# A two-layer hybrid network on one core: the norm's rows on VectorE, the last block of W in halves, another end of the last pair, updates between the projection's products

## Chip, cores and metric

The kernel runs on one core of one Trainium2 chip. The metric is the device time of one execution in microseconds (us), the median of three runs for the kernel before.

## What is computed

The input is 512 tokens of width 2048 and float32 weights. There are two layers. The first (attention and a recurrent time mix) is not touched. The second is a gated MLP with a mix along the tokens in chunks of 128, and both layers end in a post-norm and a gated projection of a side input `p`:

```python
        else:
            proj = xn @ c_w_in[j]
            u, v, g = _split(proj, (GMLP_W, GMLP_W, GMLP_W))
            oc = chunked_spatial_gating(u, v, c_ln_g[j], c_ln_b[j], c_w_s[j], c_b_s[j])
            y = (oc * jax.nn.silu(g)) @ c_w_out[j]
        h = h + rms_norm(y, norm_post[i])
        h = h + (p[i] @ ple_w_proj[i]) * jax.nn.sigmoid(h @ ple_w_gate[i])
```

In `chunked_spatial_gating`, `v` goes through a gelu and a layer norm (mean and variance, then times `c_ln_g`, plus `c_ln_b`), and each of 16 groups of 128 channels is multiplied from the left by its own lower triangle `w_s`.

## The kernel before

**Numbers.** Each float32 operand is split into a rounded part and its rest (`hi`, `lo`, typed fp32r), and a product is three matmuls: hi·hi, hi·lo, lo·hi. For a piece of W this split is one ScalarE cast (`whi`, L1384) and one VectorE subtraction (`wlo`, L1385) of 128x512; four of each can be in flight (`wsp`, four buffers). TensorE takes them in order: L1412 and L1414 need `whi`, L1413 needs `wlo`.

**Seven products.** `c_w_in` (the parts V, U, G) and the last `ple_w_gate` are multiplied by a scheme of seven products of half size in place of eight. `Pair` is two neighbouring column blocks of 512; `seven` (L1393) runs a list of (pair, product). One product is 8 k-tiles x 2 row blocks x 3 = 48 matmuls of 128x128x512. `pieces` (L1324) makes the combination of W's four quarter blocks that each product needs, in four pieces j of 128x1024 (512 KB): products 1 and 2 load; 5 adds a block onto the pieces of product 1 (called E) by an accumulating DMA from GpSimd's queue (`grow`, L1341); 6 loads four new pieces (H) and VectorE adds them to E (`add`, L1345); 3 uses H; 4 loads the last block, W's lower left one, piece by piece (L1337) and adds it to E (L1345); 7 grows H. Pieces come from a queue of nine homes, `raws`: two of the pool `wraw`, seven tiles `rq0` to `rq6`. In product 4 the loaded piece goes back to the front of that queue (`gone(g, True)`).

The order is 1, 2, 5, 6, 3, 4, 7 for a pair. The two pairs of V and the two pairs of `ple_w_gate` (called a and b here) are interleaved by `FIRST`: b1, a1, b2, a2, a5, a6, a3, a4, a7, b5, b6, and then an end that is handed in: 3, 4, 7 for V and 7, 4, 3 for the last layer. Product 1 of b isn't kept there, so b5 loads and grows.

**Side work by ticks.** `tick` counts k-tiles; `later(n, step)` puts a step n ticks ahead. `mix(g, at)` (L1490) is the mix along the tokens of group g in the U and G stages: at -11 its loads by ScalarE's queue, at -5 `norm` (four ScalarE activations L1508, one GpSimd select L1511 on `w_s`, two GpSimd tensor_tensor L1512 and L1513 for the gain and shift rows, which are broadcast), at 0 `split` (cast L1523, subtraction L1524), at +4 `mul` (three matmuls L1529 to L1531 and the gating L1533).

**Last layer.** `post_norm` (L978) runs the products with `c_w_out`, calls `next(filler)`, takes the norm's factor (`rstdB`), and runs the rest of `filler`: four groups of `ple_w_proj`, 24 matmuls each, whose results go through one of four tiles (`sg`, `sq`, two buffers each) to DRAM (`pd`, L1140 and L1141). After it come `update(q, 0)` (L1149, L1150) for eight blocks of `h`, and the operand of product 1 (`part`, L959 and L960). `flip` transposes the new `h` back to rows, 16 times, through a `sg` tile to DRAM (`rd`, L1165 and L1166). `fetch` (L1207, L1208) loads `pd` and `rd` for `emit`, on SyncE's queue (SP), on which the loads of W stand too; its slots are reused after the output has been written (L1216).

A scheduler sets the order on each engine at build time from the program's order and priorities; the `wlo`, `whi` and `add` instructions have a high one. Each engine then executes its queue in order.

```python
            else:
                tl = done = pr.E.pop(j)
                g = load(1, 0, j)
                add(tl, g)
                self.gone(g, True)
```

## Time and profile before

| | |
|---|---|
| median of 3 runs | 2293.2 us (2292.34 to 2300.28) |
| profiled execution | 2295.81 us, its span 2294.0 us |
| TensorE busy | 2230.5 us (97%) |
| VectorE busy | 1485.0 us (65%) |
| ScalarE busy | 1226.0 us (53%) |
| GpSimd busy | 289.8 us (13%) |
| mean granted TensorE clock | 0.992 |
| stages from 1376 to 1895 us | V, U and G of `c_w_in` |
| 1895 to 2074 us | products with `c_w_out` |
| 2074 to 2101 us | `ple_w_proj`, updates of h |
| 2101 to 2285 us | the fourteen products with `ple_w_gate` |

How to read it: PE is TensorE, DVE VectorE, ACT ScalarE, POOL GpSimd, SP SyncE; a suffix q is the engine's instruction queue. The view by stages gives busy time of each engine in a stretch, then the granted TensorE clock, the busy share of the DMA engines and GB/s. The view of waits gives who waited for whom, in total, how often, and the longest. In the timeline stand start, duration, engine, line, operation, and in brackets the idle time before it with what ended it. In the view of groups stand busy time in total, mean ns of one, and the idle time before.

### The profile page before, as it was taken

The numbers are of one execution on the slowest core, as the hardware profiler recorded it, in microseconds if no ns is written. First come the engines' busy times: TensorE is split into PE (matmuls) and PEld (weight loads), VectorE is DVE, ScalarE is ACT, GpSimd is POOL, SyncE is SP. The second block draws the span as 40 slices with busy tenths as digits, with TensorE's granted clock in tenths as the row PEclk, the third lists the DMA queues.
The fourth block names the chain that finished last, engine by engine and source line by source line (L and its number), as shares of the span: only waits on it lengthen the run. The fifth ranks groups of instructions, "written<-read, shape, count | busy, mean of one in ns | idle before, by whom it ended". The sixth has DMA issues, their size and how long they took to land.

```text
span 2294.0 us, 38975 instructions
## 1 busy us (share of the span) xinstructions
PE 2230.5 (97%) x14787; PEld 1823.1 (79%) x14787; DVE 1485.0 (65%) x2821; ACT 1226.0 (53%) x2510; POOL 289.8 (13%) x334
## 2 busy tenths in 40 slices
PE   8999999999999999999999999999999999998988
PEld 7878888888887888878888888877877878887767
DVE  8666667766634878862246449777787784226878
ACT  5455555555444777753344447556655654335644
POOL 2000011010100000000110112112241220010020
PEclk9999999999999999999999999999999999999999
DMA  6322232223235533343335446876676774336696
GB/s 231 90 77 78 64 86 79 73 66 84 75 97 153 154 101 98 97 149 99 97 102 172 129 120 173 209 191 150 181 207 154 215 207 134 97 104 207 173 265 196
DMA packets 298969, 311.58 MB, mean 136 GB/s; under 512 B 14701, under 2 KB 198158, under 8 KB 297758
## 3 DMA queue, kind: packets, MB, share of 16 engines
q1 hardware_dynamic: 254878, 253.52, 36.2%
q0 software_dynamic: 17408, 33.56, 8.6%
q10 hardware_dynamic: 26496, 22.03, 3.2%
q8 instruction: 116, 1.90, 0.3%
q14 instruction: 71, 0.58, 0.1%
HBM read 274.15 MB, written 34.90 MB: 135 GB/s over the span
## 4 chain that ended last, share of the span: by engine, by line
PE 78%; DVE 9%; DMA 7%; ACT 3%; issue 3%; SPq 0%; POOL 0%; ACTq 0%; DVEq 0%; POOLq 0%
PE mm L195 11%; PE mm L197 11%; PE mm L196 11%; PE mm L981 6%; PE mm L983 6%; PE mm L982 6%; PE mm L1413 5%; PE mm L1414 5%; PE mm L1412 5%; DVE wlo L1385 3%; DMA rq<-in_ple_w_gate_dram 2%; PE tm L533 1%; DMA rd<-sg 1%; DVE rq L1345 1%; PE tm L554 1%
## 5 line engine op out<-in xcount | busy, mean ns | idle before, releaser
L181 DVE TENSOR_TENSOR wlo<-raw,whi 128x512 fp32r<-128x512 f32 x464 | 331.7, 722 | 423.5 <-ACT whi L179 384.7
L179 ACT CAST whi<-raw 128x512 fp32r<-128x512 f32 x464 | 287.2, 620 | 459.1 <-PE mm L982 227.8
L196 PE MATMUL mm<-xl,whi 128*128 128x512 f32 x1088 | 427.3, 393 | 0.0
L195 PE MATMUL mm<-xh,whi 128*128 128x512 f32 x1008 | 418.4, 415 | 0.0
L197 PE MATMUL mm<-xh,wlo 128*128 128x512 f32 x1008 | 398.1, 395 | 0.0
L1384 ACT CAST whi<-rq 128x512 fp32r<-128x512 f32 x336 | 206.7, 621 | 167.9 <-PE mm L1414 91.4
L1385 DVE TENSOR_TENSOR wlo<-rq,whi 128x512 fp32r<-128x512 f32 x336 | 241.6, 730 | 77.7 <-ACT whi L1384 77.2
L196 PEld LDWEIGHTS mm<-xl,whi 128*128 128x128 f32 x1088 | 205.4, 189 | 33.5
L197 PEld LDWEIGHTS mm<-xh,wlo 128*128 128x128 f32 x1008 | 189.4, 188 | 41.7
L195 PEld LDWEIGHTS mm<-xh,whi 128*128 128x128 f32 x1008 | 190.1, 189 | 33.9
L981 PE MATMUL mm<-yl,whi 128*128 128x512 f32 x336 | 130.9, 390 | 0.0
L983 PE MATMUL mm<-yl,wlo 128*128 128x512 f32 x336 | 130.7, 389 | 0.0
L1456 POOL TENSOR_TENSOR accq<-accq,sq 128x512 f32<-128x512 f32 x42 | 56.8, 1351 | 473.1 <-ACT sq L1454 472.0
L1413 PE MATMUL mm<-wlo,xl 128*128 128x512 f32 x256 | 103.0, 402 | 11.7 <-DVE wlo L1385 11.6
L982 PE MATMUL mm<-xl,whi 128*128 128x512 f32 x288 | 112.0, 389 | 0.0
L1413 PE MATMUL mm<-wlo,yl 128*128 128x512 f32 x256 | 101.4, 396 | 10.1 <-DVE wlo L1385 10.0
L1412 PE MATMUL mm<-whi,yl 128*128 128x512 f32 x256 | 102.1, 399 | 1.1 <-ACT comb L1423 0.9
L1412 PE MATMUL mm<-whi,xl 128*128 128x512 f32 x256 | 102.7, 401 | 0.0
L1413 PE MATMUL mm<-wlo,yh 128*128 128x512 f32 x256 | 100.0, 391 | 2.2 <-DVE wlo L1385 2.2
L1414 PE MATMUL mm<-whi,xl 128*128 128x512 f32 x256 | 102.1, 399 | 0.0
L1414 PE MATMUL mm<-whi,yh 128*128 128x512 f32 x256 | 99.9, 390 | 1.1 <-DVE yh L960 1.1
L1414 PE MATMUL mm<-whi,yl 128*128 128x512 f32 x256 | 101.0, 394 | 0.0
(489 smaller groups left out, 4707.9 us busy)
## 6 DMA issues: line engine op xcount, KB each, us to landing
raw<-in_ab_w_in_dram SPq DMA_DIRECT2D x128, 512.0 KB, 3.9
rq<-in_c_w_in_dram SPq DMA_DIRECT2D x75, 512.0 KB, 6.9
rq<-in_c_w_in_dram POOLq DMA_DIRECT2D x38, 512.0 KB, 7.9
raw<-in_ple_w_gate_dram SPq DMA_DIRECT2D x36, 512.0 KB, 3.9
rq<-in_ple_w_gate_dram SPq DMA_DIRECT2D x36, 512.0 KB, 5.3
raw<-in_ab_w_out_dram SPq DMA_DIRECT2D x32, 512.0 KB, 3.7
raw<-in_c_w_out_dram SPq DMA_DIRECT2D x32, 512.0 KB, 3.8
raw<-in_c_w_in_dram SPq DMA_DIRECT2D x25, 512.0 KB, 5.8
```

Source lines behind the costliest of these rows:

```text
L179: nc.scalar.copy(hi[:, : m * n], src)
L181: self.weng.tensor_tensor(lo[:, : m * n], src, f(hi[:, : m * n]), ALU.subtract)
L195: nc.tensor.matmul(acc, hi, xhi[k], start=(k == 0), stop=False)
L196: nc.tensor.matmul(acc, hi, xlo[k], start=False, stop=False)
L197: nc.tensor.matmul(acc, lo, xhi[k], start=False, stop=(k == nk - 1))
L981: nc.tensor.matmul(accs[j], hi[:, js], xhi[k], start=(k == 0), stop=False)
L982: nc.tensor.matmul(accs[j], hi[:, js], xlo[k], start=False, stop=False)
L983: nc.tensor.matmul(accs[j], lo[:, js], xhi[k], start=False, stop=(k == nk - 1))
L1385: nc.vector.tensor_tensor(lo, src, f(hi), ALU.subtract)
L1412: nc.tensor.matmul(acc[m], xh, hi, start=(first and r == 0), stop=False, **more)
L1413: nc.tensor.matmul(acc[m], xh, lo, start=False, stop=False, **more)
L1414: nc.tensor.matmul(acc[m], xl, hi, start=False, stop=(r == 7), **more)
```

## The change

1. `norm` in `mix`: the two tensor_tensor of the gain and shift rows go from GpSimd to VectorE; `norm` is put at -4 instead of -5, `mul` at +5 instead of +4.
2. Product 4 of every pair loads the last block of W as eight 128x512 halves (256 KB) into two tiles of their own, `half0` and `half1`, and adds each to its half of E. To make room, `raws` loses `rq6`: eight homes instead of nine.
3. The end of b is 4, 7, 3 instead of 7, 4, 3, and the `fetch` ahead of product 3 is put off by three ticks.
4. In `filler` the eight `update(q, 0)` and the four `part` calls come between the groups of `ple_w_proj`, the results of which go through eight tiles `xl0` to `xl7` instead of four. The flips of the first two row blocks go through `xl` tiles, the others through `sg` and `sq`; these others come at ticks 30 to 37 instead of 20 to 34, and three later steps move by one tick.

```diff
-            self.raws = deque([(self.wraw, "raw", 2)] * 2 + [(wq, f"rq{j}", 1) for j in range(7)])
+            self.raws = deque([(self.wraw, "raw", 2)] * 2 + [(wq, f"rq{j}", 1) for j in range(6)])
...
             for g in range(4):
+                if g == 1:
+                    self.A11 = self.whole_set()
+                for q in (2 * g - 2, 2 * g - 1) if g else ():
+                    update(q, 0)
+                    if q < 4:
+                        self.part(self.A11, q, H[q, 0])
                 accs = self.dense_tm(i["ple_w_proj"][1], g * T, T, phi, plo, ps)
                 for m in range(4):
-                    pj = self.t(wp, [P, T], ("sg", "sq")[m % 2])
+                    pj = self.slot("xl", 4 * (g % 2) + m, F32)
                     nc.scalar.copy(pj, accs[m])
                     nc.scalar.dma_start(self.pd[:, m, g * T : (g + 1) * T], pj)
                 if g == 0:
                     yield
+            for q in (6, 7):
+                update(q, 0)
...
-            o = self.t(wp, [P, T], "sg")
+            o = self.slot("xl", g + 4 * m, F32) if m < 2 else self.t(wp, [P, T], ("sg", "sq")[m % 2])
...
-        order = FIRST(*pairs, (7, 4, 3))
+        order = FIRST(*pairs, (4, 7, 3))
...
                 elif prod == 3:
-                    fetch(pr.n + 1, (0, 1))
+                    self.later(3, lambda: fetch(pr.n + 1, (0, 1)))
...
                 tl = done = pr.E.pop(j)
-                g = load(1, 0, j)
-                add(tl, g)
-                self.gone(g, True)
+                for a in range(2):
+                    g = self.t(self.wq, [P, T], f"half{a}")
+                    k = 8 + 2 * j + a
+                    nc.sync.dma_start(g, pr.W[k * P : (k + 1) * P, pr.c0 : pr.c0 + T])
+                    add(tl[:, a * T : (a + 1) * T], g)
...
-                nc.gpsimd.tensor_tensor(vn, vn, row(0), ALU.mult)
-                nc.gpsimd.tensor_tensor(vn, vn, row(1), ALU.add)
+                nc.vector.tensor_tensor(vn, vn, row(0), ALU.mult)
+                nc.vector.tensor_tensor(vn, vn, row(1), ALU.add)
...
-            for n, step in ((-11, load), (-5, norm), (0, split), (4, mul)):
+            for n, step in ((-11, load), (-4, norm), (0, split), (5, mul)):
```

From the changed lines on, line numbers move by up to three: `add` is L1346 after, `wlo` L1388, the norm's rows L1515 and L1516, `fetch` L1208 and L1209, the loads of W L1338 and, for the halves, L1380.

**VectorE in the first pair of U, products 6 and 3.** Before, product 6's last add (L1345, the first row) is followed by `wlo` of the pieces, and an add of 128x1024 for product 4 comes after every two to four of them:

```order
L1345 TENSOR_TENSOR rq_3514_17144<-rq_3514_17144,rq_3577_17420 128x1024
L1385 TENSOR_TENSOR wlo_17355<-raw_17078,whi_17354 128x512
L1385 TENSOR_TENSOR wlo_17365<-raw_17078,whi_17364 128x512
L1345 TENSOR_TENSOR raw_17078<-raw_17078,rq_3601_17532 128x1024
L1385 TENSOR_TENSOR wlo_17378<-raw_17100,whi_17377 128x512
L1385 TENSOR_TENSOR wlo_17388<-raw_17100,whi_17387 128x512
L1385 TENSOR_TENSOR wlo_17401<-rq_3509_17122,whi_17400 128x512
L1385 TENSOR_TENSOR wlo_17411<-rq_3509_17122,whi_17410 128x512
L1345 TENSOR_TENSOR raw_17100<-raw_17100,rq_3606_17555 128x1024
```

After, at the same place, adds of halves stand between, and the norm's rows (`sq`, L1515 and L1516):

```order
L1346 TENSOR_TENSOR rq_3507_17102<-rq_3507_17102,half_3609_17556 128x512
L1346 TENSOR_TENSOR rq_3507_17102<-rq_3507_17102,half_3610_17559 128x512
L1515 TENSOR_TENSOR sq_17731<-sq_17731,accq_17730 128x512
L1388 TENSOR_TENSOR wlo_17412<-rq_3512_17124,whi_17411 128x512
L1388 TENSOR_TENSOR wlo_17425<-rq_3517_17146,whi_17424 128x512
L1516 TENSOR_TENSOR sq_17731<-sq_17731,accq_17730 128x512
L1388 TENSOR_TENSOR wlo_17435<-rq_3517_17146,whi_17434 128x512
L1346 TENSOR_TENSOR rq_3512_17124<-rq_3512_17124,half_3615_17582 128x512
L1388 TENSOR_TENSOR wlo_17448<-rq_3522_17168,whi_17447 128x512
L1346 TENSOR_TENSOR rq_3512_17124<-rq_3512_17124,half_3616_17585 128x512
```

The rows L1515 and L1516 are new on this engine; between two uses of the same half tile stand three `wlo`, where between two uses of the piece for product 4 stood four.

**ScalarE at the end of the projection.** Before, the casts of product 1's operand (`xh`, L959) stand behind all sixteen copies (L1140) of the projection's results:

```order
L1140 COPY sq_21689<-mm_21649 128x512
L1140 COPY sg_21692<-mm_21650 128x512
L1141 DMA pd_101<-sq_21689 128x512
L1141 DMA pd_101<-sg_21692 128x512
L1140 COPY sq_21695<-mm_21651 128x512
L959 CAST xh_4491_21698<-yh_4263_20537 128x512
L1141 DMA pd_101<-sq_21695 128x512
L959 CAST xh_4491_21698<-yh_4269_20553 128x512
```

After, the first two stand behind four copies:

```order
L1151 COPY xl_4473_21609<-mm_21567 128x512
L1151 COPY xl_4474_21612<-mm_21568 128x512
L1152 DMA pd_101<-xl_4473_21609 128x512
L179 CAST whi_21748<-raw_21746 128x512
L1152 DMA pd_101<-xl_4474_21612 128x512
L959 CAST xh_4476_21620<-yh_4287_20609 128x512
L959 CAST xh_4476_21620<-yh_4293_20625 128x512
L179 CAST whi_21764<-raw_21746 128x512
```

The other two casts follow behind eight copies.

**SP in the last pair, around a7 and b5.** Before, the loads of W (`rq`) stand between single fetches of `rd`:

```order
L1216 DMA out_dram<-xh_4724_22559 128x512
L1208 DMA xh_4724_22559<-rd_102 128x512
L1337 DMA rq_4811_22988<-in_ple_w_gate_dram 128x2x512
L1208 DMA xh_4724_22559<-rd_102 128x512
L1337 DMA rq_4816_23011<-in_ple_w_gate_dram 128x2x512
L1337 DMA rq_4821_23034<-in_ple_w_gate_dram 128x2x512
```

After, both fetches stand ahead of the last load for b5 and the four for b6:

```order
L1217 DMA out_dram<-xh_4751_22644 128x512
L1338 DMA rq_4826_23021<-in_ple_w_gate_dram 128x2x512
L1209 DMA xh_4751_22644<-rd_102 128x512 x2
L1338 DMA rq_4831_23044<-in_ple_w_gate_dram 128x2x512
L1338 DMA rq_4839_23072<-in_ple_w_gate_dram 128x2x512
```

So the two fetches have changed their places with one load.

More of the change, by code (lines that the diff above doesn't have):

```diff
@@ L1093, in rest @@
                         self.part(A11, q, xs[q, 0])
-            wq = pool("wq", 1)
-            self.raws = deque([(self.wraw, "raw", 2)] * 2 + [(wq, f"rq{j}", 1) for j in range(7)])
+            wq = self.wq = pool("wq", 1)
+            self.raws = deque([(self.wraw, "raw", 2)] * 2 + [(wq, f"rq{j}", 1) for j in range(6)])
             self.rp = pool("rp", 3)
@@ L1132, in keep, with update @@
             return last
+        def update(q, e):
+            r = self.rstdB[:, e * 256 : e * 256 + 256].unsqueeze(1).broadcast_to([P, 2, 256])
+            nc.vector.tensor_tensor(Y[q, e], Y[q, e], r, ALU.mult)
+            nc.vector.tensor_tensor(H[q, e], H[q, e], Y[q, e], ALU.add)
         def filler():
@@ L1143, in filler @@
                     yield
+            for q in (6, 7):
+                update(q, 0)
         self.post_norm(i["c_w_out"][0], npost[:, 16:32], yops, keep, ps, wp, early, filler(), None, pre)
-        def update(q, e):
-            r = self.rstdB[:, e * 256 : e * 256 + 256].unsqueeze(1).broadcast_to([P, 2, 256])
-            nc.vector.tensor_tensor(Y[q, e], Y[q, e], r, ALU.mult)
-            nc.vector.tensor_tensor(H[q, e], H[q, e], Y[q, e], ALU.add)
-        A11 = self.whole_set()
-        for q in range(4):
-            update(q, 0)
-            self.part(A11, q, H[q, 0])
-        for q in range(4, 8):
-            update(q, 0)
         def flip(g, m):
@@ L1168, in last_layer @@
         sets, x2, less, s1, s24, s3 = self.sums(H, wp)
-        sets[1] = A11
+        sets[1] = self.A11
         for q in range(4):
@@ L1194, in last_layer @@
         steps += [(19 + 3 * q, lambda q=q: s24(q, less(q))) for q in range(4)]
-        steps += [(20 + 2 * k, lambda g=g, m=m: flip(g, m)) for k, (g, m) in enumerate((g, m) for g in (2, 0, 3, 1) for m in (2, 3))]
-        steps += [(37 + q, lambda q=q: s3(q)) for q in range(4)]
-        steps += [(42, x22), (46, late_spare)]
+        steps += [(30 + k, lambda g=g, m=m: flip(g, m)) for k, (g, m) in enumerate((g, m) for g in (2, 0, 3, 1) for m in (2, 3))]
+        steps += [(38 + q, lambda q=q: s3(q)) for q in range(4)]
+        steps += [(43, x22), (47, late_spare)]
         for n, step in steps:
```

## The prediction

> **What bounds the kernel now.** I read the page first (TensorE, PE, is busy 97% of the span), then the view by stages, to see where the other 3% lie.
>
> ```profile
> 1490.00:1895.00 405.00, 384.54 (x1669) 310.44 (x1668) 315.68 (x434) 236.51 (x429) 99.24 (x82) 0.98 0.72 186
> ...
> 2074.00:2101.30 27.30, 21.15 (x92) 16.84 (x90) 24.49 (x41) 16.43 (x30) 0.00 (x0) 0.98 0.76 246
> 2101.30:2180.00 78.70, 74.51 (x333) 59.48 (x334) 58.74 (x92) 50.28 (x90) 4.80 (x4) 0.94 0.63 184
> 2180.00:2285.40 105.40, 93.75 (x397) 75.48 (x396) 83.71 (x128) 48.97 (x84) 14.44 (x12) 0.97 0.88 243
> 2285.40:2294.00 8.60, 2.07 (x10) 1.37 (x8) 4.06 (x6) 1.16 (x2) 0.00 (x0) 0.85 0.16 61
> sum 2294.00, PE 2230.49 PEld 1823.05 DVE 1485.02 ACT 1226.05 POOL 289.82; mean PE 278.81 PEld 227.88 DVE 185.63 ACT 153.26 POOL 36.23
> ```
>
> The columns are width, busy time of PE, weight load, VectorE (DVE), ScalarE (ACT) and GpSimd (POOL), then the granted TensorE clock, the DMA engines' busy share, GB/s. A stage loses its width less PE's busy time, and with it (1 - clock) x width, matmuls that ran slow. So the 405 us of V's end, U and G (call it **a**) lose 20.5 + 8.1 = 28.6; the projection (**b**) 6.15 + 0.5 = 6.7; the first part of the gate's products (**c**) 4.2 + 4.7 = 8.9; the rest of them (**d**) 11.65 + 3.2 = 14.8; the tail (**e**) is 8.6 long and holds little matmul. The clock has two digits, which in a means 2 us either way. PE's work itself stays, so a gain can only come out of these 67.6 us (28.6 + 6.7 + 8.9 + 14.8 + 8.6).
>
> Next the waits in a: who waits for whom, us in total, times, longest.
>
> ```profile
> POOL sq L1512 <- ACT sq L1508: 60.2, 12, 10.4
> ...
> PE mm L1413 <- DVE wlo L1385: 14.7, 12, 3.1
> ...
> PE mm L1530 <- DVE sg L1524: 4.2, 2, 2.3
> ```
>
> PE waits there 18.9 of its 20.5 us for VectorE, though VectorE is busy only 315.68 of 405 us (78%). So it's late at places, and its groups by shape in a show why: the means are long.
>
> ```profile
> L1385 DVE TENSOR_TENSOR wlo<-rq,whi 128x512 fp32r<-128x512 f32 x192 | 144.1, 763 | 59.1 <-ACT whi L1384 59.0
> L1385 DVE TENSOR_TENSOR wlo<-raw,whi 128x512 fp32r<-128x512 f32 x66 | 47.6, 728 | 14.8 <-ACT whi L1384 14.5
> L1345 DVE TENSOR_TENSOR rq<-rq,rq 128x1024 f32<-128x1024 f32 x19 | 29.6, 1555 | 2.3 <-DMA rq<-in_c_w_in_dram 2.0
> L1345 DVE TENSOR_TENSOR raw<-raw,rq 128x1024 f32<-128x1024 f32 x14 | 20.4, 1454 | 4.7 <-DMA rq<-in_c_w_in_dram 4.6
> ```
>
> The views by source line give min/median/max for the same instructions:
>
> ```profile
> L1385 DVE TENSOR_TENSOR wlo<-rq,whi x336: 624/685/1789, 1387.9 to 2283.0; 128x512 fp32r<-128x512 f32 x168
> ...
> L1345 DVE TENSOR_TENSOR rq<-rq,rq x31: 1210/1224/3380, 1429.5 to 2254.9; 128x1024 f32<-128x1024 f32 x31
> ```
>
> Against the medians 0.685 and 1.224 us the four groups are longer by 192 x 78 ns + 66 x 43 + 19 x 331 + 14 x 230 = 15.0 + 2.8 + 6.3 + 3.2 = 27.3 us. The timeline tells when:
>
> ```profile
> 1679.87 3.38 DVE L1345 TENSOR_TENSOR rq<-rq,rq 128x1024 f32<-128x1024 f32 x1
> ...
> 1680.39 1.76 POOL L1512 TENSOR_TENSOR sq<-sq,rstdB 128x512 f32<-128x512 f32 x1
> 1682.23 2.13 POOL L1513 TENSOR_TENSOR sq<-sq,rstdB 128x512 f32<-128x512 f32 x1
> ```
>
> The longest add is the one with the norm's GpSimd operations beside it: 3.38 - 1.22 = 2.16 us more. A stall costs twice, since matmuls after it run slow:
>
> ```profile
> 1514.47 1.23 DVE L1345 TENSOR_TENSOR rq<-rq,raw 128x1024 f32<-128x1024 f32 x1 [3.45 <-DMA raw<-in_c_w_in_dram]
> ...
> 1516.35 0.61 PE L1413 MATMUL mm<-wlo,xl 128*128 128x512 f32 x1 [2.36 <-DVE wlo L1385]
> 1516.76 0.63 PE L1414 MATMUL mm<-whi,xl 128*128 128x512 f32 x1
> ```
>
> Here VectorE waits 3.45 us for the piece of product 4, `wlo` stands behind it, PE idles 2.36 us and goes on with matmuls of 0.63 us.
>
> **Part 1, the norm's rows.** 32 operations leave GpSimd, of which the costliest group is
>
> ```profile
> L1513 POOL TENSOR_TENSOR sq<-sq,rstdB 128x512 f32<-128x512 f32 x8 | 14.1, 1767 | 0.5
> ```
>
> and come to VectorE, which does such a shape in 0.685: 32 x 0.685 = 21.9 us. With the 27.3 us of lengthening gone, its busy time in a falls by some 5 us, and the work comes in pieces of 0.685 us instead of delays of up to 2.16. Four `wlo` buffers cover about four k-ticks less what is in use, one k-tick being six matmuls of 0.23 us (384.54 us / 1669, as they overlap), 1.38 us; so about 3 x 1.38 = 4.1 us. One norm, two rows of 0.685 with a `wlo` between, stays far below. Its later place (-4 for -5) and `mul` at +5 leave the split and the mix's matmuls a tick (1.38 us) nearer and further, which I cost at nothing as ScalarE, busy 236.51 of 405 us, hides it; without that cover PE's 4.2 us of waits for the split stay. I expect most of the 18.9 us to go, and the slow clock with it. Bounds for a: 0 to 28.6, and below nothing if VectorE, which works in order, waits itself (a rival). I take two thirds, **19**, since the stalls that DMA causes (part 2) are among the 28.6.
>
> The Trainium skill, page "SBUF — State Buffer", section "Who interferes with whom", says that a VectorE operation with two SBUF inputs and a GpSimd operation that reads SBUF exclude each other, the second to issue being blocked until the first ends. The trace agrees in the row of 3.38 us. By that rule alone the most that can be freed is the GpSimd time, an estimate of 32 x 1.77 = 57 us of VectorE, where the medians give 27.3.
>
> **Part 2, halves.** Product 4 of each of the pairs gets 8 loads and 8 adds for 4 and 4. On VectorE a pair of halves costs 2 x 0.685 - 1.224 = 0.15 us more, 8 products x 4 x 0.15 = 4.7 us over all, hidden in VectorE's idle 22% of a (and 21.7 us of d); without that cover they would be 4.7 us of PE. SyncE issues 32 loads more, of 0.32 us by the row at 2220.05 below, 10 us over a span in which it mostly waits; but a half that waits for its tile holds up the loads queued behind it on SyncE, as a piece that waited for its home did before. No load of 256 KB of W is in the trace. The nearest rows, of the DMA views (the first two in a, the third in c and d), with us to landing at the end:
>
> ```profile
> rq<-in_c_w_in_dram SPq DMA_DIRECT2D x68, 512.0 KB, 7.1
> ...
> sq<-vd ACTq DMA_DIRECT2D x16, 256.0 KB, 3.0
> ...
> xh<-rd SPq DMA_DIRECT2D x12, 256.0 KB, 9.8
> ```
>
> Before, four pieces in one home take 4 x (7.1 + 1.22) = 33 us against two products of 11.0 us (48 x 0.23) in which they are added: late, as at 1514.47. After, two tiles give four rounds of two halves: 4 x (3.0 + 0.69) = 15 at one end, 4 x (9.8 + 0.69) = 42 at the other. I take about half of 7.1 plus a bit, 4.5: 4 x 5.2 = 21 against 22, just in time: the first row has the same source and queue, and its time is mostly bytes. The gain is in a's 19 and in d; the one home less (eight) makes H's loads start later by one piece and is weighed in the range.
>
> **Part 3, other end of b, and part 4's flips.** The waits of c:
>
> ```profile
> DVE sg L1268 <- DMA rd<-sg: 7.7, 3, 3.1
> ...
> ACT sg L1165 <- DMA rd<-sg: 5.9, 3, 3.2
> ```
>
> ScalarE and VectorE both wait, in order, until the flips' tiles are written out, 13.6 us in all; `whi` and `wlo` stand behind them. Eight flips now have tiles of their own, so half of the waits have no cause; the other eight move to ticks 30 to 37, four tiles for eight flips one tick apart. Of c's loss of 8.9, about 2.5 is the slow stretch after b's stall and belongs to b; of the 6.4 left I take **2** (ends -2 and 6.4), since VectorE gets work of b, below.
>
> In d the largest single stall, in the timeline of SyncE and VectorE:
>
> ```profile
> 2220.05 0.32 SPq L1208 DMA_DIRECT2D xh<-rd  x1
> 2220.48 1.34 SPq L1337 DMA_DIRECT2D rq<-in_ple_w_gate_dram  x1
> ...
> 2229.91 1.23 DVE L1345 TENSOR_TENSOR rq<-rq,rq 128x1024 f32<-128x1024 f32 x1 [9.02 <-DMA rq<-in_ple_w_gate_dram]
> ```
>
> A load of W for b6 stands behind a fetch of `rd` whose slot isn't free until 2220.05, and the add waits 9.02 us for it. After, both fetches stand ahead of one more load, so SyncE can still block there. But product 4's own loads, which came through the same queue with 512 KB each and gave their home back late, are halves with tiles of their own, the outputs that free the slot come from a VectorE that is late less often, and the fetch for product 3 is put off by three ticks (4.1 us), past loads of W. The waits of VectorE in d:
>
> ```profile
> DVE rq L1345 <- DMA rq<-in_ple_w_gate_dram: 12.5, 4, 9.0
> ```
>
> Of d's 14.8 I take **8** (ends 0 and 14.8), about half of it: I see the cause weakened, not removed.
>
> In e the change loses. In 7, 4, 3 the last product has beside it the two blocks that product 4 completes, six VectorE operations (L1443, L1212, L1214); in 4, 7, 3 it has the four blocks that product 7 completes, fourteen (L1436 and L1438 too). Eight more at 0.685 are 5.5 us, in a product of 11.0 us whose sixteen `wlo` already take 11.0 at that median, some of them ahead of it. They stand mostly behind the last `wlo`, so PE isn't held, but the outputs of the last block are. I take **-2** (ends -5.5 and 0), as some fit into gaps.
>
> **Part 4, updates between the products.** ScalarE in b:
>
> ```profile
> 2093.20 0.59 ACT L1140 COPY sg<-mm 128x512 f32<-128x512 f32 x1 [2.34 <-DMA pd<-sg]
> ...
> 2101.34 0.80 PE L1412 MATMUL mm<-whi,xh 128*128 128x512 f32 x1 [6.19 <-ACT xh L959]
> ```
>
> The copies wait for tiles to be written to `pd`, the casts of the first product's operand stand behind them, and PE idles 6.19 us. After, eight tiles end the wait, and two casts stand behind four copies, the others behind eight. Late next is VectorE: 24.49 of 27.3 us busy, and its 24 updates don't shrink. b and c together give it 24.5 + 58.7 = 83 us of work in 106 us, or in 98 after a gain of 8: 85%. I take **8** of 6.7 + 2.5 = 9.2 (ends 0 and 9.2).
>
> The sum is 19 + 8 + 2 + 8 - 2 = 35. The profiled execution took 2295.81 us, 1.8 outside its span; less 35 it's 2260.8. It lies 2.6 above the median of the runs, so I forecast 2293.2 - 35 = **2258**. With all upper ends, 28.6 + 9.2 + 6.4 + 14.8 + 0 = 59, it is 2234.
>
> **The rivals.** First, the trouble moves: VectorE is full from b to c, the late flips come in a burst, and halves wait for their own tiles in a. Then a gains 9, b 8, c -4, d 4, e -2: 15, so **2278**. For it speaks VectorE's 90% in b; against, that most of its work there may be late without PE waiting.
>
> Second, transfers bound it: the DMA engines are busy 0.72 of a and 0.88 of d, 92.8 of 105.4 us, the bytes don't change, and halves land no sooner than whole pieces (toward 9.8). Then a gains 5, b 5, c 0, d 2, e -2: 10, so **2283**. Against it, 0.72 leaves room. The Trainium skill, "DMA: Bandwidth & Descriptors", section "Measured (HBM→SBUF, 128 partitions, SWDGE, issued from GpSimd)", asks for transfers of 1 MiB or more, which speaks against halves and for this rival; no run here shows 1 MiB.
>
> Third, slower: the norm's rows now wait on VectorE, in order, for ScalarE (L1508), where GpSimd waited 60.2 us in 12 waits, 5.0 each; every `wlo` queued behind them waits as well, and PE for those. With 4.1 us of cover the short ones vanish; if half of the 60.2 reaches PE and a's 19 is lost, the others' 16 remain: 2293.2 + 30 - 16 = **2307**. It decides from 27.5 us that reach PE (16 + 11.5). Against it: GpSimd came early because it had nothing else to do, VectorE will come later, and the norm's activations take part of a tick each.
>
> **How the numbers follow.** Measurement can tell 0.5%, 11.5 us: below 2281.7 is faster, above 2304.7 slower. My forecast has 0.55, the rivals 0.20, 0.15 and 0.10. Faster is 0.55, two thirds of the first rival and a quarter of the second: 0.55 + 0.13 + 0.04 = 0.72; slower the third, 0.10; the same 0.18. The range runs from all upper ends, 2234, up through both rivals with half of the second's 10 gone, 2288; it leaves out the third rival and the edges, under 0.2.
>
> **What would show it.** Right: in a no `wlo` beyond 1 us, adds of 128x1024 near 1.22, PE's waits for `wlo` there below 6; no ScalarE wait for `pd`, first product's matmul under 1 us late; in d no VectorE wait of 9 us. Wrong: VectorE waits for L1508 or for the gain and shift rows of over 4 us with PE waiting behind; adds of halves waiting for DMA in every product 4; PE's idle time in c above 4.2.

## The result and the profile after

The changed kernel takes 2284.4 us (median of 6 runs, 2277.9 to 2286.1), the kernel before 2297.9 (6 runs, 2292.3 to 2301.1). The ratio is 0.9939, with a 95% interval of 0.9918 to 0.9960: 14 us faster, where 35 were forecast. The time lies inside the range, near its upper end. By the gain it is the first rival (15 us); by the time alone the second (2283) is as near as the first (2278), since the kernel before took 4.7 us more over these six runs than over the three that the forecast started from. By the prediction's own line for "faster", 2281.7 us, 2284.4 counts as the same, to which it gave 0.18; by the ratio the gain is 0.6%, with an interval that includes its 0.5%.

Where the 14 us came from is read off two kinds of row. The first are the starts of TensorE's work by source line, in the form "first to last start". The first matmuls of V's product (L1412 before, L1415 after) and the first matmul of the products with `c_w_out` (L981 with `xh`) bound the stage of V, U and G. Before:

```profile
L1412 PE MATMUL mm<-whi,xh x128: 388/389/796, 1384.7 to 2134.3; 128*128 128x512 f32 x128
...
L981 PE MATMUL mm<-xh,whi x48: 389/389/478, 1894.1 to 1994.6; 128*128 128x512 f32 x48
```

After:

```profile
L1415 PE MATMUL mm<-whi,xh x128: 389/389/794, 1386.5 to 2117.6; 128*128 128x512 f32 x128
...
L981 PE MATMUL mm<-xh,whi x48: 389/389/478, 1885.2 to 1985.8; 128*128 128x512 f32 x48
```

So this stage went from 1894.1 - 1384.7 = 509.4 us to 1885.2 - 1386.5 = 498.7, a gain of **10.7**. (It starts 1.8 us later after; nothing ahead of it was changed.)

The second kind is the fourteen products with `ple_w_gate`, counted off in TensorE's timeline, 48 matmuls each. The time from a product's first matmul to the next one's (the last: to its own last matmul), in us; flips stand inside them:

| | b1 | a1 | b2 | a2 | a5 | a6 | a3 | a4 | a7 | b5 | b6 | three last | sum |
|---|---|---|---|---|---|---|---|---|---|---|---|---|---|
| before | 17.3 | 16.4 | 13.9 | 12.8 | 11.5 | 11.3 | 12.9 | 12.3 | 12.4 | 20.1 | 10.9 | 34.1 | 185.7 |
| after | 18.4 | 13.7 | 10.9 | 12.2 | 18.7 | 11.7 | 10.9 | 11.8 | 11.3 | 20.1 | 13.1 | 34.0 | 186.8 |

The wait ahead of the first of them fell from 6.6 to 0.2 us, counted from start to start (the stretch from `c_w_out` to there gained **6.3**), the first five take 2.0 more, the rest 0.9 less (113.9 to 113.0), and the tail from the last matmul's start to the end grew from 6.9 to 8.5 (**-1.6**). 10.7 + 6.3 - 2.0 + 0.9 - 1.6, less the 1.8 ahead of it all, is 12.5, which is the difference of the spans, 2294.0 - 2281.5.

The stages after, to be held against those of before (same columns; a first, then the projection, b1 to a5, and the rest):

```profile
1491.80:1886.10 394.30, 380.98 (x1668) 308.29 (x1667) 305.11 (x486) 236.99 (x430) 53.74 (x50) 0.99 0.73 190
...
2065.10:2086.15 21.05, 21.05 (x93) 17.08 (x91) 18.42 (x32) 14.39 (x26) 0.00 (x0) 1.00 0.66 197
2086.15:2160.00 73.85, 66.69 (x305) 53.77 (x304) 63.58 (x101) 49.35 (x86) 4.81 (x4) 0.94 0.73 218
2160.00:2273.20 113.20, 103.53 (x434) 82.05 (x432) 85.65 (x136) 53.28 (x92) 14.46 (x12) 0.96 0.84 227
```

TensorE idles 394.30 - 380.98 = 13.3 us in a, where it was 20.5, none in the projection, 7.2 from b1 to a5, 9.7 in the rest. What it waits for in a:

```profile
ACT sq L1511 <- DMA sq<-vd: 20.0, 6, 5.6
...
ACT whi L1387 <- DMA vd<-comb: 7.3, 1, 7.3
...
DVE rq L1346 <- DMA half<-in_c_w_in_dram: 6.3, 12, 1.1
PE mm L1415 <- ACT whi L1387: 6.0, 2, 3.5
...
PE mm L1533 <- DVE sg L1527: 3.8, 5, 1.6
...
PE mm L1416 <- DVE wlo L1388: 3.3, 5, 1.0
```

The waits for `wlo` fell from 14.7 to 3.3 us. In their place TensorE waits 6.0 us, in two pieces, for `whi`: ScalarE, not VectorE, is late. VectorE's groups show that part 1 did to VectorE what was forecast: `wlo` and the adds are back at their medians, and the norm's rows cost what was put in.

```profile
L1388 DVE TENSOR_TENSOR wlo<-rq,whi 128x512 fp32r<-128x512 f32 x202 | 136.5, 687 | 61.7 <-ACT whi L1387 59.9 <-DMA rq<-in_c_w_in_dram 1.3
...
L1346 DVE TENSOR_TENSOR rq<-rq,rq 128x1024 f32<-128x1024 f32 x10 | 12.2, 1220 | 0.0
...
L1515 DVE TENSOR_TENSOR sq<-sq,rstdB 128x512 f32<-128x512 f32 x8 | 5.5, 685 | 0.1
```

### The profile page after: what moved, and what is told of

It reads as the page before. It is cut to its first block, busy times and chain, and to the rows that moved or that the text cites. A ratio compares the mean times of both kernels' runs of the same rounds, so it can differ in the third digit from the quotient of the medians.

```text
span 2281.5 us, 39072 instructions
## 1 busy us (share of the span) xinstructions
PE 2228.9 (98%) x14787; PEld 1822.5 (80%) x14787; DVE 1476.4 (65%) x2885; ACT 1226.8 (54%) x2510; POOL 244.2 (11%) x302
## 4 chain that ended last, share of the span: by engine, by line
PE 82%; DVE 7%; DMA 6%; ACT 3%; issue 2%; SPq 0%; ACTq 0%; DVEq 0%; POOLq 0%
PE mm L195 11%; PE mm L197 11%; PE mm L196 11%; PE mm L982 6%; PE mm L983 6%; PE mm L981 6%; PE mm L1415 6%; PE mm L1416 6%; PE mm L1417 6%; DVE wlo L1388 2%; PE tm L533 1%; DMA sq<-vd 1%; DVE rq L1346 1%; PE tm L554 1%; DMA rq<-in_ple_w_gate_dram 1%
## 5 line engine op out<-in xcount | busy, mean ns | idle before, releaser
L1388 DVE TENSOR_TENSOR wlo<-rq,whi 128x512 fp32r<-128x512 f32 x340 | 230.0, 687 | 86.3 <-ACT whi L1387 84.2
L981 PE MATMUL mm<-yl,whi 128*128 128x512 f32 x336 | 130.9, 390 | 0.0
L1415 PE MATMUL mm<-whi,yh 128*128 128x512 f32 x256 | 101.3, 396 | 3.5 <-ACT whi L1387 3.5
L1415 PE MATMUL mm<-whi,xl 128*128 128x512 f32 x256 | 101.5, 396 | 2.5 <-ACT whi L1387 2.5
L1415 PE MATMUL mm<-whi,yl 128*128 128x512 f32 x256 | 101.3, 396 | 0.9 <-ACT whi L1387 0.9
L1417 PE MATMUL mm<-whi,yh 128*128 128x512 f32 x256 | 100.4, 392 | 0.0
```

The source lines that it names most:

```text
L981: nc.tensor.matmul(accs[j], hi[:, js], xhi[k], start=(k == 0), stop=False)
L1388: nc.vector.tensor_tensor(lo, src, f(hi), ALU.subtract)
L1415: nc.tensor.matmul(acc[m], xh, hi, start=(first and r == 0), stop=False, **more)
L1417: nc.tensor.matmul(acc[m], xl, hi, start=False, stop=(r == 7), **more)
```

## The experiments

The ratios below are to the kernel before, in runs on the same chip, with their intervals; the stage times are from one profiled execution each. How far those differ where an edit changes nothing: the start of V lies between 1381.9 and 1386.5 us, V, U and G took 496.5 to 500.3 us in the five executions with the change's own code there, and in the four with the change's own last layer a1 took 12.6 to 13.8 us and b5 20.1 to 20.6. So two totals are told apart only where their intervals are. Edits are given against the changed kernel, if nothing else is said. The change itself: 0.9939, a 498.7, gate's products 186.8.

**Which part made the gain.** First the norm's rows back on GpSimd:

```diff
-                nc.vector.tensor_tensor(vn, vn, row(0), ALU.mult)
-                nc.vector.tensor_tensor(vn, vn, row(1), ALU.add)
+                nc.gpsimd.tensor_tensor(vn, vn, row(0), ALU.mult)
+                nc.gpsimd.tensor_tensor(vn, vn, row(1), ALU.add)
```

> The changed kernel with the norm's 32 rows back on GpSimd, all else as in the change (its place at -4 and mul at +5 too). Measured from the first matmul of V to the first one with c_w_out, U, V and G take 509.4 us before and 498.7 after. Theory A, GpSimd's operations lengthen VectorE's and that was the gain there: the means of wlo come back from 687 to over 720 ns, PE's waits for wlo there from 3.3 to over 10 us, and the stretch to 505 to 511 us; total 2290 to 2296. Theory B, the halves made the gain: the stretch stays at 496 to 502 us, total 2281 to 2287.

Measured: 2298.7 us, ratio 1.0009 (1.0000 to 1.0019); V, U and G took 517.3 us. Theory A, and more than it asked: without its first part the change gains nothing, and this stage is 18.6 us longer than with it. VectorE's groups in this run, by shape:

```profile
L1388 DVE TENSOR_TENSOR wlo<-rq,whi 128x512 fp32r<-128x512 f32 x203 | 149.5, 747 | 66.5 <-ACT whi L1387 66.0
...
L1346 DVE TENSOR_TENSOR rq<-rq,rq 128x1024 f32<-128x1024 f32 x10 | 14.3, 1434 | 0.0
...
L1441 DVE TENSOR_TENSOR comb<-comb,comb 128x512 f32<-128x512 f32 x10 | 9.0, 903 | 0.0
L1446 DVE TENSOR_TENSOR comb<-mm,comb 128x512 f32<-128x512 f32 x11 | 7.5, 680 | 0.0
```

The reader should compare the last two: same shape, same engine, same stage. The one that reads two tiles of SBUF takes 903 ns (684 in the change, without GpSimd's rows), the one that reads one of its inputs from PSUM (`mm`) 680 (682), while `wlo` is at 747 again. This agrees with the Trainium skill, "SBUF — State Buffer", section "Who interferes with whom", by which a VectorE operation with two SBUF inputs contends with a GpSimd operation that reads SBUF, and one with at most one, outside VectorE's modes that use two ports, does not. TensorE's waits in the same run also tell why it is longer than before's 509.4: 8.3 us go to the split's `sg`, in two waits (before 4.2), and 5.1 to `whi` (before 0.5). The rows themselves had ended over 9 us ahead of both waits for `sg`; VectorE had waited 1.6 and 2.4 us there for a half of product 4. So not all of the 18.6 us is the price of the rows.

```profile
PE mm L1416 <- DVE wlo L1388: 10.1, 11, 2.5
...
PE mm L1533 <- DVE sg L1527: 8.3, 2, 4.8
```

Then part 1 alone, on the kernel before (rows on VectorE, at -5, whole pieces, the old last layer):

> The kernel before with part 1 alone: the norm's two rows on VectorE, at -5 as before, product 4 in whole pieces, nothing else changed. With all the rest of the change but the rows on GpSimd the total was 2298.7, no gain. Theory A: this alone brings the whole gain, V, U and G at 498 to 504 us against 509.4, total 2282 to 2288. Rival: the parts need each other (halves free VectorE for the rows), the stretch stays over 505 us, total 2289 or more.

Measured: 2285.9 us, ratio 0.9958 (0.9945 to 0.9971), V, U and G 497.8 us, the gate's products 185.9, the wait ahead of them 6.9. Theory A: two lines bring 11.6 us in their stage, and their total can't be told from that of the whole change. TensorE still waits there 7.0 us for `wlo` and 5.9 for `sg`, but only 2.2 for `whi`.

**Halves or whole pieces.**

```diff
-                for a in range(2):
-                    g = self.t(self.wq, [P, T], f"half{a}")
-                    k = 8 + 2 * j + a
-                    nc.sync.dma_start(g, pr.W[k * P : (k + 1) * P, pr.c0 : pr.c0 + T])
-                    add(tl[:, a * T : (a + 1) * T], g)
+                g = load(1, 0, j)
+                add(tl, g)
+                self.gone(g, True)
```

(and `rq6` is back).

> The changed kernel with product 4's last block in whole pieces of 512 KB again, through nine homes. Theory A (GpSimd was the cause): V, U and G stay at 496 to 502 us, total within 4 us of the changed kernel's 2284. Theory B (the halves made the gain): VectorE's adds of product 4 wait for DMA by over 3 us at a time, the stretch goes to 505 to 511 us, total 2291 to 2296. In the gate's products, 186.8 us from first to last matmul after and 185.7 before, B would add 3 us or more, A nothing.

Measured: 2284.5 us, ratio 0.9945 (0.9930 to 0.9960); V, U and G 501.1 us, gate's products 185.8. Theory A. The halves do land as I hoped: in V, U and G, by the view of DMA issues of the changed kernel,

```profile
rq<-in_c_w_in_dram SPq DMA_DIRECT2D x44, 512.0 KB, 5.8
...
half<-in_c_w_in_dram SPq DMA_DIRECT2D x46, 256.0 KB, 2.8
```

256 KB take 2.8 us, and the longest wait of an add for one is 1.1 us. (The rule of 1 MiB that the prediction weighed from the Trainium skill, "DMA: Bandwidth & Descriptors", section "Measured (HBM→SBUF, 128 partitions, SWDGE, issued from GpSimd)", did not decide here: halves cost no time in this stage.) They remove a stall that the run with whole pieces has in TensorE's timeline,

```profile
1515.93 0.80 PE L1414 MATMUL mm<-wlo,xl 128*128 128x512 f32 x1 [3.91 <-DVE wlo L1386]
```

and another wait takes its place, below. (In the last run of this document, with whole pieces and an edit of `vd`'s loads, TensorE waits nowhere in this stage over 1.4 us, so whole pieces alone don't make that stall.)

**The norm's place.**

```diff
-            for n, step in ((-11, load), (-4, norm), (0, split), (5, mul)):
+            for n, step in ((-11, load), (-5, norm), (0, split), (4, mul)):
```

> The changed kernel with norm at -5 and mul at +4 again, the rows staying on VectorE. After, PE waits in this stage 6.0 us for whi and 3.8 for the split's sg, which it did not before at this size (0.5 and 4.2). Theory C, the place a tick later makes them: the waits for sg and whi fall below 5 together, the stretch of V, U and G shortens by 3 to 6 us. Theory D, ScalarE waits in its queue for the loads of vd whatever the tick: both remain, the stretch stays within 2 us of 498.7.

Measured: 2279.2 us, ratio 0.9915 (0.9894 to 0.9936), which overlaps the change's; V, U and G took 503.2 us in the profiled execution, with a wait of TensorE for the split's `sg` that no other run has at this length:

```profile
1689.59 0.80 PE L1533 MATMUL mm<-sg,w 128*128 128x512 f32 x1 [9.68 <-DVE sg L1527]
```

Ahead of it ScalarE had waited 10.51 us, up to 1686.82, for a load of `vd` to land, with the casts for VectorE behind it. That is the wait of theory D, but neither theory's numbers came. The four executions took 2273.6, 2275.5, 2282.9 and 2283.2 us, and the profiled one is the last of these; so what the place is worth stays undecided.

**ScalarE's new wait.** ScalarE's timeline in the changed kernel, late in V (which ends at 1546.9):

```profile
1514.18 1.14 ACT L1387 CAST whi<-rq 128x512 fp32r<-128x512 f32 x2
1522.14 0.34 ACTq L1502 DMA_DIRECT2D sq<-vd  x1
1522.58 0.62 ACT L1387 CAST whi<-rq 128x512 fp32r<-128x512 f32 x1 [7.25 <-DMA vd<-comb]
```

The load of `vd` for the first group can't be issued until `vd` has been written. It stands in ScalarE's queue, so ScalarE does nothing for 7.25 us, the next `whi` is late, and so is TensorE:

```profile
1523.25 0.80 PE L1415 MATMUL mm<-whi,yh 128*128 128x512 f32 x1 [3.52 <-ACT whi L1387]
```

This wait came with part 2. In the changed kernel the last write of `vd` that the load needs is issued 127.2 us after V's first matmul (1386.5), behind an operation of VectorE (L1446) that stands behind adds of halves, and the load follows 8.4 us after the write:

```profile
1512.25 0.68 DVE L1446 TENSOR_TENSOR comb<-mm,comb 128x512 f32<-128x512 f32 x1
```

```profile
1513.72 0.37 ACTq L1479 DMA_DIRECT2D vd<-comb  x1
```

With whole pieces (the run above) the same write is issued 121.9 us after V's first matmul, and the load follows 2.7 us after it (the DMA engines' share is 0.52 in the 4 us from 1504, and 1.10 in the changed kernel's 8 us from 1514):

```profile
1504.73 0.37 ACTq L1477 DMA_DIRECT2D vd<-comb  x1
...
1507.41 1.33 ACTq L1500 DMA_DIRECT2D sq<-vd  x2
```

All nine executions with halves and this load on ScalarE's queue have the wait at this place, of 5.9 to 8.3 us; the three with whole pieces (the kernel before, part 1 alone, the run above) don't. That the adds put L1446 so late is read off VectorE's order; no run moves it alone.

The edit:

```diff
-                nc.scalar.dma_start(vn, self.vd[:, g])
+                (nc.sync if g < 2 else nc.scalar).dma_start(vn, self.vd[:, g])
```

> The changed kernel with the loads of vd for the first two groups on SyncE's queue instead of ScalarE's. After, ScalarE waited 7.25 us at 1522 to issue them until vd had been written, its casts whi stood behind, and PE idled 3.52 us. Theory I, that wait in ScalarE's queue is the cause: the stall goes, V, U and G take 493 to 496 us instead of 498.7. Theory J, the wait only moves: SyncE holds the loads of W behind it, VectorE's adds or the casts wait for them, and the stretch stays within 2 us of 498.7 or grows.

Measured: 2273.2 us, ratio 0.9918 (0.9904 to 0.9933); V, U and G 493.0 us. Theory I: the stage is 5.7 us shorter, for a stall of 3.5 and the slow matmuls after it. V's fourteen products alone, counted like those of the gate, took 158.4 to 161.6 us in the seven executions with the change's V, and 154.5 to 155.1 in the three with halves and this edit. The intervals of the totals still overlap. TensorE's waits for `whi` went from 6.0 to 1.3 us:

```profile
PE mm L1416 <- DVE wlo L1388: 4.3, 9, 0.9
PE mm L1533 <- DVE sg L1527: 3.5, 5, 1.0
PE mm L1415 <- ACT whi L1387: 1.3, 3, 0.7
```

**The flips.** In the changed kernel TensorE itself waits in the stretch b1 to a5, for the copies that empty the flips' PSUM tiles; before, no such wait stood there:

```profile
PE mm L1164 <- ACT xl L1166: 2.4, 1, 2.4
...
PE mm L1164 <- ACT sq L1166: 2.0, 2, 1.7
PE mm L1164 <- ACT sg L1166: 1.9, 1, 1.9
```

First all flips as they were, tile and ticks:

```diff
-            o = self.slot("xl", g + 4 * m, F32) if m < 2 else self.t(wp, [P, T], ("sg", "sq")[m % 2])
+            o = self.t(wp, [P, T], "sg")
...
-        steps += [(30 + k, lambda g=g, m=m: flip(g, m)) for k, (g, m) in ...
+        steps += [(20 + 2 * k, lambda g=g, m=m: flip(g, m)) for k, (g, m) in ...
```

> The changed kernel with all sixteen flips through sg at their old ticks (20 to 34 by twos), and the three later steps back by a tick; the projection's order and its eight tiles stay. After, a5 took 18.7 us from first to first matmul where it took 11.5 before, and PE idles in it on flips. Theory E, the burst at ticks 30 to 37 costs these 7 us: a5 takes 11 to 13 us, the gate's products go from 186.8 to 179 to 183 us. Theory F, the flips' tiles were right and the loss comes wherever the flips stand, since their writes and VectorE are full: the waits for rd come back (6 us or more on VectorE and ScalarE), the gate's products take 185 to 190 us.

Measured: 2285.7 us, ratio 0.9952 (0.9937 to 0.9967); the gate's products 192.5 us, b1 21.5, a5 15.2. Theory F for this edit, though its 185 to 190 us were exceeded: a5 gains 3.5, b1 loses 3.1, and VectorE and ScalarE wait for `rd` again (6.3 and 4.2 us). So I took the ticks alone (the second line of the diff, and the three later steps):

> The changed kernel with the last eight flips at ticks 20 to 34 by twos again (three later steps back by a tick), but through sg and sq, and the first eight through xl, as in the change. In the run with all flips through sg at the old ticks the gate's products took 192.5 us, a5 alone 15.2 instead of 18.7, the first product 21.5 instead of 18.4. Theory E, the burst is the fault, and the tiles were right: a5 takes 11 to 13 us, the two or three products before it 1 us more each, the gate's products 181 to 185 us. Theory F, the eight flips cost the same wherever they stand: 186 us or more.

Measured: 2276.5 us, ratio 0.9930 (0.9914 to 0.9947); the gate's products 181.6 us, a5 11.5. Theory E: the gate's products are 5.2 us shorter, though the intervals of the totals overlap. The gain was 7.2 us in a5, and 5.6 were given back in a4, which took 17.4 instead of 11.8: there TensorE waits 3.5 us for the operand `yh` (L960). Another 4.2 came in b5, which took 15.9 instead of 20.1 though nothing in it was changed; perhaps since a longer a4 leaves its loads more time. From a5 to b5 the products took 84.5 us in the change and 78.0 here, and 79.0 and 78.8 in the first two runs of the last part, which have the same flips.

**The stall in b5.** Four edits. The fetches on another queue:

```diff
-                nc.sync.dma_start(pj[n, m], self.pd[:, m, n * T : (n + 1) * T])
-                nc.sync.dma_start(res[n, m], self.rd[:, m, n * T : (n + 1) * T])
+                nc.gpsimd.dma_start(pj[n, m], self.pd[:, m, n * T : (n + 1) * T])
+                nc.gpsimd.dma_start(res[n, m], self.rd[:, m, n * T : (n + 1) * T])
```

> The changed kernel with every fetch of pd and rd on GpSimd's queue instead of SyncE's, so that no load of W stands behind a fetch that waits for its slot. After, b5 took 20.1 us up to b6's first matmul, 9.2 more than 48 matmuls need, and the loads of W stood behind two fetches until 2200.15. Theory G, the order of SyncE's queue makes that stall: b5 takes 11 to 14 us, the gate's products 178 to 182 us instead of 186.8. Theory H, the transfers do: the DMA engines are busy over 1.0 from 2176 to 2216, b5 stays at 18 to 22 us, the gate's products at 184 us or more.

Measured: 2279.7 us, ratio 0.9950 (0.9934 to 0.9967); b5 18.8 us, b6 14.7 (13.1 in the change), gate's products 185.4. G's numbers did not come: b5 and b6 together took 33.5 us as against 33.2. But the edit is not clean. The accumulating loads of b5 are issued from GpSimd's queue, and two of them now stood behind fetches that waited for their slots:

```profile
2195.02 0.54 POOL L1209 DMA_DIRECT2D xh<-rd  x1 [2.09 <-DMA out_dram<-xh]
2195.56 1.26 POOL L1342 DMA_DIRECT2D rq<-in_ple_w_gate_dram  x1
2200.99 0.58 POOL L1209 DMA_DIRECT2D xh<-rd  x1 [4.17 <-DMA out_dram<-xh]
2201.57 1.23 POOL L1342 DMA_DIRECT2D rq<-in_ple_w_gate_dram  x1
```

What speaks for H is that SyncE issued the loads for b6 from 2190.76 on, 9.8 us ahead of b5's first matmul (4.9 in the change), and that the one of them whose landing the trace has took 18.0 us:

```profile
rq<-in_ple_w_gate_dram SPq DMA_DIRECT2D x6, 512.0 KB, 18.0
```

Most of `pd` left out:

```diff
-                nc.sync.dma_start(pj[n, m], self.pd[:, m, n * T : (n + 1) * T])
+                nc.sync.dma_start(pj[n, m][:, 0:16], self.pd[:, m, n * T : n * T + 16])
...
-            nc.vector.tensor_tensor(src, src, pj[n, m], ALU.mult)
+            nc.vector.tensor_tensor(src, src, pj[n, m][:, 0:1].broadcast_to([P, T]), ALU.mult)
```

> The changed kernel, leaving out all but 16 of the 512 columns of every fetched block of pd (the result is multiplied by column 0 alone); the order of SyncE's queue stays. It takes some 240 KB of each of 16 fetches from the DMA engines, of which 12 (2.9 MB) stand from 2176 on. Theory H, transfers bound b5: b5 takes 11 to 15 us, the gate's products 176 to 182 us. Theory G, SyncE's order does: b5 stays at 18 us or more, the gate's products at 184 us or more.

Measured: 2272.4 us, ratio 0.9921 (0.9904 to 0.9937); b5 18.5 us, gate's products 181.5. Neither: b5 as G said (1.6 us less), the sum of the products as H said (5.3 us less, with b6 and the next product 1.1 us less each). So I took away bytes in b5 itself, its accumulating load:

```diff
-                if j not in pr.E:
+                kept = j in pr.E
+                if not kept:
                     pr.E[j] = load(0, 0, j)
                 tl = pr.E[j]
-                grow(tl, 0, 1, j)
+                if kept:
+                    grow(tl, 0, 1, j)
```

> The changed kernel, leaving out the accumulating load of the second block in product 5 of a pair whose product 1 isn't kept (b5, in V and in the last layer): 2 MB less for the DMA engines just where b5 and b6 need 6 MB, while the loads for b6 still can't be issued before a7 has given back its homes. With 3 MB of pd left out, b5 only went from 20.1 to 18.5 us. Theory H, the transfers of b5 and b6 bound it: b5 takes 11 to 14 us, the gate's products 178 to 183 us. Theory K, the late issue (homes, and the slots of the fetches ahead) bounds it: b5 stays at 17 us or more.

Measured: 2271.0 us, ratio 0.9897 (0.9884 to 0.9911); b5 14.6 us, gate's products 180.8. This is near H, but it takes out a step of a chain as well as bytes. The accumulate kept, of 16 columns only, tells these apart:

```diff
+                else:
+                    nc.gpsimd.dma_start(view(tl)[:, :, 0:16], block(0, 1, j)[:, :, 0:16], accum_op=ALU.add)
```

> The changed kernel with the accumulating load in product 5 of b cut to 16 of its 512 columns, in V and in the last layer (the rest of the second block is left out); the chain of load, wait on GpSimd and accumulate stays as it was, only 2 MB less for the DMA engines. Without that load altogether b5 took 14.6 us instead of 20.1. Theory H, the bytes bound b5: b5 takes 13 to 16 us again. Theory L, the chain of a late load and an accumulate behind it bounds it: b5 takes 18 us or more.

Measured: 2272.0 us, ratio 0.9902 (0.9887 to 0.9917); b5 14.6 us again, gate's products 179.2. Theory H. The five loads of W in question are issued no earlier than in the change, 5.5 us ahead of b5's first matmul there and 5.6 here. SyncE's rows, of the change and then of this run:

```profile
2200.15 3.44 SPq L1338 DMA_DIRECT2D rq<-in_ple_w_gate_dram  x5
```

```profile
2195.67 3.77 SPq L1338 DMA_DIRECT2D rq<-in_ple_w_gate_dram  x5
```

But they land sooner. The busy share of the DMA engines in the change (next to last column) in the 40 us up to b6's first operand, and just ahead of them:

```profile
2172.00:2176.00 4.00, 4.00 (x19) 3.34 (x18) 4.00 (x8) 2.57 (x5) 1.88 (x2) 1.00 0.57 123
2176.00:2216.00 40.00, 32.61 (x139) 25.57 (x138) 24.67 (x40) 17.39 (x31) 7.75 (x7) 0.96 1.07 286
```

and VectorE's first add for b6, in the change and with the thin accumulate:

```profile
2214.28 1.23 DVE L1346 TENSOR_TENSOR raw<-raw,rq 128x1024 f32<-128x1024 f32 x1 [7.33 <-DMA rq<-in_ple_w_gate_dram]
```

```profile
2204.39 1.23 DVE L1346 TENSOR_TENSOR raw<-raw,rq 128x1024 f32<-128x1024 f32 x1 [4.24 <-DMA rq<-in_ple_w_gate_dram]
```

For 40 us the DMA engines are full (1.07), at 286 GB/s; 2 MB less shorten b5 by 5.5 us, which at that rate are 2 x 1.05 MB / 286 GB/s = 7.3 us of transfers. So 5.5 of the stall's 9.2 us are the transfers. 3.7 us (14.6 less 10.9) remain, and whether these are the homes or the rest of the bytes stays open: with nine homes and all bytes b5 took 17.0 us (the run with whole pieces), and product 4 behind b6 then 16.2 instead of 12.5.

Not all bytes cost the same. GpSimd's queue (q0) carries the accumulating loads alone in the change, SyncE's (q1) the plain loads and the outputs. Over the gate's products, with packets, MB and the share of the 16 DMA engines' time:

```profile
q1 hardware_dynamic: 14501, 27.09, 44.3%
q0 software_dynamic: 4352, 8.39, 25.8%
```

A megabyte takes 1.6% on q1 and 3.1% on q0, 1.9 times as much. It is the accumulating and not the queue: in the run with the fetches on GpSimd's queue, over the same products, q0 has 7.87 MB more of plain loads for 12.1 points more, 1.5% each:

```profile
q0 software_dynamic: 6752, 16.26, 37.9%
q1 hardware_dynamic: 10082, 19.02, 30.6%
```

So the 2 MB of accumulating loads count for about 4 of plain ones, an estimate from these rows; that is part of why they did more for b5 than 3 MB of `pd`.

**What helped, together.** The vd loads and the spread flips:

> The changed kernel with both edits that helped alone: the first two loads of vd on SyncE's queue, and the last eight flips at ticks 20 to 34 by twos through sg and sq. They act in different stages, so that they should add: V, U and G 493 us (498.7 less 5.7), the gate's products 181 to 183 us (186.8 less 5), the total 2284 - 11 = 2271 to 2275. If one only moved the other's wait, 2276 to 2282.

Measured: 2269.9 us, ratio 0.9893 (0.9878 to 0.9909); V, U and G 498.2 us in the profiled execution, as ScalarE's second wait was there this time (TensorE 3.2 us for `whi`), the gate's products 179.9. The total is as expected. With the old end of b:

```diff
-        order = FIRST(*pairs, (4, 7, 3))
+        order = FIRST(*pairs, (7, 4, 3))
```

> The same as the run with both edits, and the last layer's end of b in the order 7, 4, 3 again, the fetch ahead of product 3 still put off by three ticks. By the term of the forecast for the tail (-2, measured 6.9 us before and 8.5 to 8.6 after, from the last product's last matmul to the end) it gives 1.5 to 2 us back: tail 6.8 to 7.1 us, total 2 us under the run with 4, 7, 3. Rival: the order 4, 7, 3 spares a wait of product 7 or 4 that comes back, the last four products take 2 us more and the total is the same or longer.

Measured: 2267.6 us, ratio 0.9885 (0.9869 to 0.9901); tail 6.9 us instead of 8.5. The tail is as the theory has it; but the gate's products took 182.4 us, 2.5 more than in the run before, with b5 at 21.2 instead of 17.9, and the intervals of the two totals overlap. So what the old end is worth in all is not shown. This is the fastest version found, 1.15% under the kernel before. With whole pieces and nine homes:

> The best run so far (first two loads of vd on SyncE's queue, the last eight flips at ticks 20 to 34, end 7, 4, 3) with product 4's block in whole pieces through nine homes. In the changed kernel the halves were worth 2.4 us in V, U and G, and with nine homes b5 took 17.0 instead of 20.1 us. Theory M, with the other stalls gone the halves matter: V, U and G grow from 491.6 to 496 us or more, total 2270 to 2275. Theory N, the ninth home gives as much in b5 as the halves take: total within 2 us of 2267.6.

Measured: 2271.4 us, ratio 0.9901 (0.9885 to 0.9918); V, U and G 492.9 us, b5 17.8, gate's products 182.8. M's 496 us did not come, N's 2 us were exceeded (3.8), and the intervals overlap: whether the halves are worth anything isn't settled, and it is little.

## Why the forecast was wrong

The direction was right and the sum was not: 35 us forecast, 14 measured. Most of what is missing is in a (8.3 us) and d (7.1), then in c (4.0). By the forecast's own terms:

- **a, 19 forecast, 10.7 measured.** The mechanism of part 1 was right: rows on GpSimd or on VectorE differ by 11.6 us in the old kernel, and by 18.6 in the changed one, where other waits were longer too. The step that failed is "I expect most of the 18.9 us to go, and the slow clock with it". TensorE's waits for VectorE fell from 18.9 to 7.1 us (3.3 for `wlo`, and 3.8 for the split, which I had said would stay without cover), but 6.0 us of waits for ScalarE took their place, and I had named no late engine behind VectorE. The larger of these two is behind the load of `vd` that could not be issued (5.7 us of the stage with the slow matmuls), the other behind a wait of 5.6 us for such a load to land. "Loads by ScalarE's queue" stood in the description, and the row of 7.9 us for the loads of `vd` in the waits of before; I did not ask what these loads wait for once adds of halves stand ahead of what `vd` is made from. V did not end earlier (160.4 us for its products, 159.0 before). The third rival's wait (VectorE for the norm's activations) did not come.
- **The row of 3.38 us.** I read it as agreeing with the rule quoted beside it, that the second to issue is blocked. That add had started 0.52 us ahead of GpSimd's operation and was longer all the same. So the row shows that the two hinder each other, not which of them is blocked.
- **Halves, within a and d.** The row of 7.1 us to landing is for all of V, U and G; in the 405 us of a alone the same view has 5.6 (55 loads), so the old side of my sum was 4 x (5.6 + 1.22) = 27 us, not 33. The estimate of 4.5 for a half was too high (2.8). Halves ended waits for late pieces, brought the wait for `vd`, and took a home from b5; the totals are 2284.4 with them and 2284.5 without.
- **b, 8 forecast, 6.3 measured.** Right: the wait of 6.6 us ahead of the first product went. The 2.5 us of slow matmuls I had added were not gained, since b1 still took 18.4 us; TensorE waits in it 3.2 us for copies of the flips.
- **c, 2 forecast, -2.0 measured.** The failing step is "half of the waits have no cause" for the flips. The waits of VectorE and ScalarE for `rd` did go (13.6 to 0.4 us), but eight flips in a row held up TensorE, through the copies out of PSUM: its idle time there was 7.2 us, over the 4.2 that I had named as a sign of being wrong. I had written of the burst and put its price into the lower end (-2) only. Spreading the flips shortened a5 by 7.2 us and the products from a5 to b5 by 5.4 to 6.5.
- **d, 8 forecast, 0.9 measured.** The step "I see the cause weakened" had the wrong cause. I took the stall of b5 for one of SyncE's order. At least 5.5 of its 9.2 us are transfers, as 2 MB less in b5 showed; b5 took 20.1 us before and after. The fetches off SyncE's queue changed b5 and b6 by 0.3 us, in a run that is not clean. The second rival had this, and gave d 2.
- **e, -2 forecast, -1.6 measured.** Right for the tail, and the old order gives it back (6.9).

So the first rival comes near the sum, a 9, b 8, c -4, d 4, e -2: 15. It had 0.20. That is luck in part: of its mechanisms only the burst of flips came. The adds of halves waited at most 1.1 us in a, where the time went to ScalarE's queue.

## What to carry to other kernels

When a shared resource makes the critical engine's helper late, the lengthened groups show it (27.3 us here), but the stage gained less (11.6 with the two lines alone). Before booking the stalls, look which queue is next, and above all which DMA issues stand in the queue of an engine that computes: here one such issue held ScalarE for 7.25 us. Look also at what a part of the change puts ahead of other work in an engine's queue, even where its own waits are short, as with the adds of halves. Before charging a stall behind a late load to the queue's order, look whether the DMA engines have idle time there; here their share was 1.07, and leaving out 2 MB gave 5.5 us. And of a change with several parts, try the smallest alone: here the gain of two lines could not be told from that of all four parts.

## What the runs showed of the hardware

With GpSimd's tensor operations beside them, VectorE's operations with two SBUF inputs took 903 and 747 ns on the mean, those with one PSUM input 680, in the same stage of the same run; without them 684, 687 and 682. A megabyte of accumulating loads took 1.9 times the DMA engines' time of a megabyte of plain ones. Two MB of accumulating loads left out in b5 were worth 5.5 us there; 3 MB of plain loads left out, half of them issued 12 to 23 us ahead of b5, 1.6 us in b5 and 5.3 over all the gate's products.
